# Layer 1's modulation weights in a staging ring of their own, taken in pairs of column chunks

## The chip, the cores and the metric

The kernel runs on one core of a Trainium2 chip. The metric is device time in microseconds (us): from the first to the last instruction of one execution, as a median over several runs. Names of engines: PE is TensorE, DVE is VectorE, ACT is ScalarE, POOL is GpSimd, SP is SyncE, which here only issues DMAs.

## The reference

Two layers of a trunk work on 256 latent and 256 context tokens of width 2048, all in float32. Layer 0 mixes tokens by pooling windows, layer 1 by neighbourhood attention; each is followed by a gated feed-forward block of width 5504. Before each sub-layer the tokens are normalised and modulated, and the modulation is what the change is about:

```python
silu_c, silu_cc = jax.nn.silu(c), jax.nn.silu(c_ctx)
for i in range(DEPTH):                                     # DEPTH = 2
    ml = (silu_c  @ w_mod[i] + b_mod[i]).reshape(B, 6, 1, D)   # for the latent tokens
    mc = (silu_cc @ w_mod[i] + b_mod[i]).reshape(6, 1, 1, D)   # for the context tokens
    a_lat = modulate(rms_norm(h, norm1_g[i]), ml[:, 0], ml[:, 1])
    a_ctx = modulate(rms_norm(hc, norm1_g[i]), mc[0], mc[1])
    ...                                                    # mixer i
    h = h + ml[:, 2] * y_lat
    h = h + ml[:, 5] * conv_ffn(modulate(rms_norm(h, norm2_g[i]), ml[:, 3], ml[:, 4]), ...)
    if not last:
        ...                                                # the same for the context tokens hc
```

`w_mod[i]` is 2048 by 12288 and is read once per layer: 24 chunks of 512 columns, 4 MB each. Of layer 1 the first 8 chunks (shift and scale of the first norm) are needed for both streams, and the other 16 for the latent tokens alone.

## The kernel before, in words

The program is written in order, and a scheduler that simulates its time line sets the order of the instructions on each engine; every engine then runs its own list strictly in that order. So does SP: a DMA that waits for a free buffer holds up all DMAs behind it.

Float32 products are made on PE as three passes. A weight tile of 128x1024 float32 (512 KB) is loaded into a staging buffer; ACT copies it, rounded, to a tile `h` (line 142), DVE subtracts that to get the remainder, tile `l` (line 144), and PE multiplies `h` and `l` with the two halves of the activations. I call the copy and subtraction of one tile its split. Split tiles lie in a ring of three pairs plus one (`whp`, `whx`), so the tile that is split for PE lies at most three tiles ahead of the one that PE reads.

Staging buffers come from one pool of six (`wst`), which `load` and `stage` hand out in turn to whatever asks next. While a buffer is in use, the load that is to come into it waits on SP.

The feed-forward block of layer 0 fills the span from about 450 to 1760 us. It runs over 43 slices `f` of 128 columns; the products of the first eight are made during the mixer. From the ninth on, `gu0(f)` makes the gate and up products (lines 651 to 653), with two tiles `wg` and two tiles `wu`, and `gate0` turns them into an activation `act` (lines 337 to 352). After four slices, `down0` multiplies the four slices before those with the down weights (lines 675 to 677), in four groups `mg` of two tiles `wd`; ACT scales the result into `dy` (line 687) and POOL adds it to the residual `hl`, `hc` (line 688). A period of four slices and one down step is 24 weight tiles.

Beside that block, DVE computes the modulation of layer 1. `mod_pieces` is a generator of 96 pieces, and `gu0` and `down0` draw one at each pair of weight tiles (`next(pump)`). A piece loads two tiles `wm` through the same staging pool and does on DVE, for each of four rows of 128 inputs, `macc = wm * c + macc` (lines 219 and 221), 128x512, for one stream or for both. After four pieces a chunk is summed: DVE transposes blocks of 32 and reduces them (lines 228 and 229, tile `modr`), PE sums the four quarters with one matmul with a constant tile `quad` (line 165, `modt`), and DVE adds the bias (line 181). That matmul is issued with high priority in the midst of the block's matmuls.

In layer 0 the same weights go through PE (`mod_pe`), also out of the staging pool.

Of the kernel before, what the change touches and what calls it, by code (L numbers as in the profile page):

```python
# [34 lines left out]
RATE = 20  # L35
PMAX = 30

NRH = 3
# [19 lines left out]
def kernel(ctx: ExitStack, tc: tile.TileContext, xT, cxT, wmod, wg, wu, wd, wp,  # L58
                         wq, wv, wo, vec, cc, rope, inv, strips, out):
    nc = tc.nc  # L60
    main = ctx.enter_context(tc.tile_pool(name="main", bufs=1))
    wst = ctx.enter_context(tc.tile_pool(name="wst", bufs=6))
    whp = ctx.enter_context(tc.tile_pool(name="whp", bufs=3))
# [41 lines left out]

    rooms = [None] * 6

    def lend(ks):

        rooms[:] = [r for r in rooms if r is None or r in ks] + [k for k in ks if k not in rooms]  # L110

    def stage(name):

        r = rooms.pop(0)
        rooms.append(r)
        if r is not None:
            return ap0.tile([P, 1024], F32, tag=f"A{r}", name=name)
        return wst.tile([P, 1024], F32, tag="wst", name=name)

# [39 lines left out]

    def quarter_sum(x, n, name):  # L160


        with tc.high_priority():
            ps = bank("d", f"{name}s")
            nc.tensor.matmul(ps[:, : 16 * n].rearrange("p (k s) -> p k s", s=n), quad, x, start=True, stop=True)
        v = ps[:, : 16 * n].rearrange("p (i b s) -> p i b s", b=4, s=n)
        return [v[32 * b : 32 * b + 32, :, b, :] for b in range(4)]

    def finish_mod(l, ch, streams, src):

        mt = src[0] if len(src) == 1 else main.tile([P, 4, 2], F32, name=f"modT{l}_{ch}")
        n = len(streams)
        which, q = divmod(ch, 4)

        def dup(name, a):
            return V(name)[:, a : a + 8].rearrange("p (i s) -> p i s", s=2)[:, :, 0:n]

        bias = dup(f"bm_{l}", 8 * ch)
        for b, v in enumerate(src):
            own = slice(32 * b, 32 * b + 32) if len(src) > 1 else slice(0, P)  # L180
            nc.vector.tensor_tensor(mt[own, :, 0:n], v, bias[own], op=ALU.add)
        if which in (1, 4):
            nc.vector.scalar_tensor_tensor(mt[:, :, 0:n], mt[:, :, 0:n], 1.0, dup(f"g{1 if which == 1 else 2}_{l}", 8 * q),
                                           op0=ALU.add, op1=ALU.mult)
        modT[l, ch] = mt

    def mod_pe(l, ch, sc, pool):

        ps = bank("m", f"mod{l}_{ch}")
        for g in range(4):  # L190
            ts = load(lambda a, b: wmod[l, ch, g, :, a:b], 2048, f"wm{l}_{ch}_{g}")
            for j in range(4):
                nc.tensor.matmul(ps[32 * j : 32 * j + 32, :], sc[:, 4 * g + j, :],  # L193
                                 ts[j // 2][0][:, 512 * (j % 2) : 512 * (j % 2) + 512],
                                 start=(g == 0), stop=(g == 3), tile_position=(0, 32 * j))
            if g == 3:
# [9 lines left out]
        finish_mod(l, ch, both, [r])  # L206

    def mod_pieces(todo, pool):

        for l, ch, streams in todo:  # L210
            acc = {s: pool.tile([P, 512], F32, tag=f"macc{s}", bufs=1, name=f"macc{s}_{l}_{ch}") for s in streams}
            for g in range(4):
                ts = load(lambda a, b: wmod[l, ch, g, :, a:b], 2048, f"wm{l}_{ch}_{g}")
                for j in range(4):
                    k = 4 * g + j
                    w = ts[j // 2][0][:, 512 * (j % 2) : 512 * (j % 2) + 512]
                    for s in streams:
                        if k == 0:
                            nc.vector.tensor_scalar(acc[s], w, sc2[:, k, s : s + 1], None, op0=ALU.mult)
                        else:  # L220
                            nc.vector.scalar_tensor_tensor(acc[s], w, sc2[:, k, s : s + 1], acc[s],  # L221
                                                           op0=ALU.mult, op1=ALU.add)
                if g == 3:
                    n = len(streams)
                    r = pool.tile([P, 16, 2], F32, tag="modr", bufs=2, name=f"modr_{l}_{ch}")[:, :, 0:n]
                    for s in streams:
                        t = f0.tile([P, 512], F32, tag="t2", name=f"modu{s}_{l}_{ch}")
                        nc.vector.transpose(t, acc[s])
                        nc.vector.tensor_reduce(out=r[:, :, s], in_=t.rearrange("p (k r) -> p k r", r=32), axis=AX.X,
                                                op=ALU.add)  # L230
                yield
            finish_mod(l, ch, streams, quarter_sum(r, n, f"modt_{l}_{ch}"))

# [62 lines left out]
    with ExitStack() as ph0:  # L296
# [16 lines left out]
        PART = {}  # L313
        sc = p0.tile([P, KT, 32], F32, name="sc")
        nc.gpsimd.memset(sc, 0.0)
        nc.vector.tensor_copy(sc[:, :, 0:2], sc2)
        wsh = p0.tile([P, 2, NS, 2], F32, name="wsh")
# [17 lines left out]
        def gate0(f, pg, pu):  # L335
# [10 lines left out]
            if f == NS - 1:  # L346
                a = [mp.tile([P, 512], F32R, tag=f"macc{j}", bufs=1, name=f"act_{f}_{j}") for j in range(2)]
            else:
                a = act_tile(f"act_{f}", F32R)
                a = [a[:, 0], a[:, 1]]  # L350
# [8 lines left out]
        with ExitStack() as phs:  # L359
            st = phs.enter_context(tc.tile_pool(name="st", bufs=2, reuse_waits="tile"))  # L360
            for g in range(4):
                nc.sync.dma_start(hl[:, 4 * g : 4 * g + 4, :], xT[:, 4 * g : 4 * g + 4, :])
# [272 lines left out]
        extra.append(whx)  # L635
        two = [(1, q, both) for q in range(8)]
        one = [(1, q, (0,)) for q in range(8, 24)]
        pump = mod_pieces([x for t in zip(two, one[::2], one[1::2]) for x in t], mp)
# [20 lines left out]
        def down0(c, fs, acts, after=None):  # L659
            n = len(fs)  # L660
            last = c == len(chunks) - 1
            for mg in range(4):
                parts = split(load(lambda a, b: wd[0, mg, :, fs[0] + a // 512 : fs[0] + b // 512, :], 512 * n, f"wd0_{c}_{mg}"),
                              f"wd0_{c}_{mg}")
                if c > 1:
                    next(pump, None)
                    if mg % 2 and c < 3:
                        next(pump, None)
                for m in range(4):
# [48 lines left out]
        down0(*prev)  # L718
        for _ in pump:
            pass  # L720
        extra.clear()

# [506 lines left out]
```

## Time and profile before

| | |
|---|---|
| three runs | 3149.84, 3158.88, 3161.52 us; median 3158.88 |
| span of the profiled execution | 3167.2 us, 8.3 us above that median (no other time of that execution is given) |
| PE busy | 3058.2 us (97%), 15082 matmuls |
| DVE busy | 2031.6 us (64%) |
| ACT, POOL busy | 1364.5 us (43%), 940.3 us (30%) |
| bytes moved | 559.72 MB, 177 GB/s over the span |

The shares are those of the whole span, in which stages with other limits lie. PE's busy time counts matmuls that overlap, so what counts of PE is the time in which it has none: some 109 us in all. The windows that follow are in us from the span's start.

### The profile page before, as it was taken

How to read it: one execution, taken by the hardware profiler on the slowest of the kernel's cores; microseconds unless marked ns; L12 is line 12 of the kernel's file. 1: busy time of each engine (PE TensorE's matmuls, PEld its weight loads, DVE VectorE, ACT ScalarE, POOL GpSimd, SP SyncE). 2: the span in 40 equal slices, each digit the busy share in tenths (PEclk: the TensorE clock that was granted, in tenths of full speed). 3: DMA queues.
4: the chain of work that ended last, by engine and by line, in shares of the span. 5: the costliest groups of instructions: out<-in, count | busy, mean ns of one | idle time of the engine just before them, and what ended most of it. 6: DMA issues, size and time to landing. Idle time of an engine off the chain costs nothing.

```text
span 3167.2 us, 40924 instructions
## 1 busy us (share of the span) xinstructions
PE 3058.2 (97%) x15082; PEld 2419.7 (76%) x15082; DVE 2031.6 (64%) x2865; ACT 1364.5 (43%) x2219; POOL 940.3 (30%) x846
## 2 busy tenths in 40 slices
PE   5999999999999999999999999999999999999998
PEld 2565558887877777777778788778778888888887
DVE  4444774287685876758585674564777666666666
ACT  3333454323233332323234453343545655556665
POOL 2011213204042240404133000000002477667776
PEclk9999999999999999999999999999999999999999
DMA  9877663265564656555464233333345555555553
GB/s 360 322 283 278 214 225 102 90 226 181 178 195 159 204 160 204 163 185 189 159 205 132 95 119 103 104 108 101 108 140 180 178 193 180 199 184 183 180 185 115
DMA packets 161545, 559.72 MB, mean 177 GB/s; under 512 B 17600, under 2 KB 22208, under 8 KB 161344
## 3 DMA queue, kind: packets, MB, share of 16 engines
q1 hardware_dynamic: 161344, 557.10, 53.2%
q8 instruction: 119, 1.95, 0.2%
q14 instruction: 82, 0.67, 0.1%
HBM read 554.93 MB, written 2.10 MB: 176 GB/s over the span
## 4 chain that ended last, share of the span: by engine, by line
PE 69%; DMA 13%; DVE 11%; issue 3%; POOL 3%; ACT 1%; SPq 0%; DVEq 0%; POOLq 0%; ACTq 0%
DMA wm<-wmod 12%; DVE macc L221 5%; PE g L781 5%; PE u L781 4%; PE d L826 4%; PE d L677 3%; PE mod L193 3%; PE d L675 3%; PE d L676 3%; PE g L782 2%; PE u L782 2%; PE d L827 2%; PE k L951 2%; PE q L969 2%; PE k L953 2%
## 5 line engine op out<-in xcount | busy, mean ns | idle before, releaser
L221 DVE SCALAR_TENSOR_TENSOR macc<-wm,sc,macc 128x512 f32<-128x512 f32 x480 | 410.0, 878 | 231.8 <-DMA wm<-wmod 227.3
L688 POOL TENSOR_TENSOR hl<-hl,dy 128x256 f32<-128x256 f32 x160 | 163.7, 1023 | 941.9 <-ACT dy L687 941.0
L838 POOL TENSOR_TENSOR hl<-hl,dy 128x256 f32<-128x256 f32 x320 | 321.3, 1037 | 45.4 <-ACT dy L836 43.8
L687 ACT ACTIVATE dy<-d,modT 128x256 f32<-128x256 f32 x320 | 133.2, 470 | 172.2 <-PE d L677 157.0
L688 POOL TENSOR_TENSOR hc<-hc,dy 128x256 f32<-128x256 f32 x160 | 179.8, 1124 | 0.0
L344 ACT ACTIVATE sg<-g 128x512 f32<-128x512 f32 x43 | 27.2, 632 | 309.3 <-DVE g L341 309.3
L193 PE MATMUL mod<-wm,sc 128*32 128x512 f32 x768 | 137.3, 632 | 22.4 <-DVE n1q L255 19.3
L925 POOL TENSOR_TENSOR rk<-rk,rp 128x256 f32<-128x256 f32 x16 | 13.8, 861 | 366.0 <-DVE rk L924 302.4
L836 ACT ACTIVATE dy<-d,modT 128x512 f32<-128x512 f32 x160 | 103.6, 686 | 29.9 <-PE d L827 27.5
L428 POOL TENSOR_TENSOR pf<-ws,inv 128x256 f32<-128x256 f32 x32 | 26.4, 847 | 208.7 <-DVE ws L420 187.7
L144 DVE TENSOR_TENSOR wd_2l<-wd,wd_2h 128x1024 fp32r<-128x1024 f32 (+1 forms) x44 | 57.5, 1312 | 47.0 <-ACT wd_2h L142 46.1
L677 PE MATMUL d<-act,wd_0l 128*128 128x512 f32 x172 | 71.0, 413 | 16.4 <-DVE wd_0l L144 16.4
L805 DVE TENSOR_TENSOR actb<-sgb,actb 128x256 fp32r<-128x256 f32 x43 | 70.0, 1628 | 21.1 <-ACT actb L804 20.3
L193 PEld LDWEIGHTS mod<-wm,sc 128*32 128x32 f32 x768 | 23.5, 111 | 76.9 <-issue 63.0
L144 DVE TENSOR_TENSOR wd_0l<-wd,wd_0h 128x1024 fp32r<-128x1024 f32 (+1 forms) x44 | 54.3, 1235 | 34.0 <-ACT wd_0h L142 33.3
L1011 ACT ACTIVATE sb<-sb,nm 128x512 f32<-128x512 f32 x64 | 46.2, 722 | 63.1 <-DVE nm L1007 61.4
L142 ACT CAST wd_0h<-wd 128x1024 fp32r<-128x1024 f32 (+1 forms) x44 | 45.3, 1031 | 63.4 <-PE g L652 32.2
L676 PE MATMUL d<-act,wd_0h 128*128 128x512 f32 x172 | 70.0, 407 | 0.0
L675 PE MATMUL d<-act,wd_0h 128*128 128x512 f32 x172 | 69.7, 406 | 0.0
L677 PE MATMUL d<-act,wd_1l 128*128 128x512 f32 x172 | 68.1, 396 | 0.5 <-DVE wd_1l L144 0.5
L676 PE MATMUL d<-act,wd_2h 128*128 128x512 f32 x172 | 68.0, 395 | 0.0
L675 PE MATMUL d<-act,wd_3h 128*128 128x512 f32 x172 | 68.0, 395 | 0.0
(1762 smaller groups left out, 10063.2 us busy)
## 6 DMA issues: line engine op xcount, KB each, us to landing
wm<-wmod SPq DMA_DIRECT2D x384, 512.0 KB, 5.4
wd<-wd SPq DMA_DIRECT2D x168, 512.0 KB, 4.6
wg<-wg SPq DMA_DIRECT2D x156, 512.0 KB, 4.2
wu<-wu SPq DMA_DIRECT2D x156, 512.0 KB, 4.8
wv<-wv SPq DMA_DIRECT2D x32, 512.0 KB, 3.7
wk<-wq SPq DMA_DIRECT2D x32, 512.0 KB, 3.9
wq<-wq SPq DMA_DIRECT2D x32, 512.0 KB, 3.8
wo<-wo SPq DMA_DIRECT2D x32, 512.0 KB, 3.8
```

Source lines behind the costliest of these rows:

```text
L144: eng.tensor_tensor(lo[:, :n], t[:, :n], hi[:, :n].bitcast(F32), op=ALU.subtract)
L193: nc.tensor.matmul(ps[32 * j : 32 * j + 32, :], sc[:, 4 * g + j, :], ts[j // 2][0][:, 512 * (j % 2) : 512 * (j % 2) + 512], start=(g == 0) ...
L221: nc.vector.scalar_tensor_tensor(acc[s], w, sc2[:, k, s : s + 1], acc[s], op0=ALU.mult, op1=ALU.add)
L675: nc.tensor.matmul(ps, hi[:, o : o + P], xh, start=(i == 0), stop=False)
L676: nc.tensor.matmul(ps, hi[:, o : o + P], xl, start=False, stop=False)
L677: nc.tensor.matmul(ps, lo[:, o : o + P], xh, start=False, stop=(i == n - 1))
L687: nc.scalar.activation(y[:, s], ps[:, T * s : T * s + T], AF.Copy, scale=M(0, 5, k, s))
L688: nc.gpsimd.tensor_tensor(h_of(s)[:, k, :], h_of(s)[:, k, :], y[:, s], op=ALU.add)
L781: nc.tensor.matmul(ps, hi[:, c : c + P], flat(B[k]), start=(k == 0), stop=False)
L782: nc.tensor.matmul(ps[:, T:], lo[:, c : c + P], B[k][:, 0], start=False, stop=(k == KT - 1))
L826: nc.tensor.matmul(ps, hi[:, o : o + P], flat(acts[i]), start=(i == 0), stop=False)
L838: nc.gpsimd.tensor_tensor(hl[:, k, :], hl[:, k, :], y[:, q], op=ALU.add)
```

## The change

The six staging tiles become two rings of three in the same pool: tag `wst` for block weights, tag `wm` for layer 1's modulation weights. In layer 0's mixer and from the attention on, `stage` still walks through all six; from the first `pump()` until the modulation is done, block weights have the three of `wst` alone.

Of the 24 chunks, the first 8 (both streams) still go one at a time (`single`): eight tiles of 128x1024, four DVE instructions of 128x512 per tile. The other 16 go two at a time (`pair`): a tile now holds 512 columns of two chunks for one row of inputs, and one DVE instruction of 128x1024 takes it. The DVE instructions for the products go from 512 to 384, the loads stay 192 of 512 KB. One single and one pair alternate.

Each draw from the generator no longer yields one piece of two tiles: `pump()` adds 2.9 to an account, and draws tiles that cost 1.0 (pair) or 2.3 (single) until it is used up.

The transposed sums of all chunks are kept in one tile `sums`, and the matmul with `quad` is done twice at the end (`spread`, 128x256 each), not 24 times. The bias is then added by 12 DVE instructions in place of 96. The results lie in one tile `m1`.

The padded input `sc` for layer 0's modulation moves to a pool that is closed earlier, and the two accumulators `macc0`, `macc1` become one tile of twice the width.

```diff
-    wst = ctx.enter_context(tc.tile_pool(name="wst", bufs=6))
+    wst = ctx.enter_context(tc.tile_pool(name="wst", bufs=3))
...
-    rooms = [None] * 6
+    rooms = ["wst"] * 3 + ["wm"] * 3
...
-    def mod_pieces(todo, pool):
-
-        for l, ch, streams in todo:
-            acc = {s: pool.tile([P, 512], F32, tag=f"macc{s}", bufs=1, name=f"macc{s}_{l}_{ch}") for s in streams}
...
-            finish_mod(l, ch, streams, quarter_sum(r, n, f"modt_{l}_{ch}"))
+    def mod_pieces(pool):
+
+        sums = pool.tile([P, 32, 16], F32, name="modr")
...
+        def pair(a):
+
+            acc = pool.tile([P, 2, 512], F32, tag="macc", bufs=1, name=f"macc_{a}")
+            for k in range(KT):
+                t = wst.tile([P, 1024], F32, tag="wm", name=f"wm1_{a}_{k}")
+                w = t.rearrange("p (c n) -> p c n", c=2)
+                g, kk = divmod(k, 4)
+                nc.sync.dma_start(w, wmod[1, a : a + 2, g, :, 512 * kk : 512 * kk + 512].rearrange("c p n -> p c n"))
...
+                    nc.vector.scalar_tensor_tensor(acc, w, sc2[:, k, 0:1], acc, op0=ALU.mult, op1=ALU.add)
+                yield 1.0
+            for c in range(2):
+                fold(acc[:, c], a + c + 8, f"{a + c}")
...
+        def single(ch):
...
+                    yield 2.3
...
+        for n in range(8):
+            yield from single(n)
+            yield from pair(8 + 2 * n)
+        yield 0.5
+        spread(0, 16, 0, "modt_a")
+        spread(16, 16, 8, "modt_b")
+        yield 0.5
...
+        def pump():
+
+            rooms[:] = ["wst"] * 3
+            owed[0] += PACE
+            while owed[0] > 0.0:
+                owed[0] -= next(pieces, 1e9)
...
                 if c > 1:
-                    next(pump, None)
-                    if mg % 2 and c < 3:
-                        next(pump, None)
+                    pump()
```

On SP, the loads at the end of slice 23 and the start of the down step that follows (`wd_4` is its weight tile, `wm_13` and `wm_3` are modulation chunks) stood like this before:

```order
L126 DMA wu_23_0_7466<-wu 128x1024
L126 DMA wu_23_1024_7468<-wu 128x1024
L126 DMA wm_13_1_0_7478<-wmod 128x1024
L126 DMA wm_13_1_1024_7480<-wmod 128x1024
L126 DMA wd_4_0_0_7545<-wd 128x1024
L126 DMA wd_4_0_1024_7547<-wd 128x1024
L126 DMA wm_13_2_0_7557<-wmod 128x1024
L126 DMA wm_13_2_1024_7559<-wmod 128x1024
L126 DMA wd_4_1_0_7637<-wd 128x1024
L126 DMA wd_4_1_1024_7639<-wd 128x1024
```

Two and two alternate there. In the changed kernel the same place reads as follows (`wm_12_3` is the fourth of the sixteen tiles of the pair of chunks 12 and 13):

```order
L127 DMA wd_4_0_0_7411<-wd 128x1024
L215 DMA wm_12_3_7343<-wmod 128x2x512
L127 DMA wd_4_0_1024_7413<-wd 128x1024
L215 DMA wm_12_4_7346<-wmod 128x2x512
L215 DMA wm_12_5_7349<-wmod 128x2x512
L215 DMA wm_12_6_7423<-wmod 128x2x512
L127 DMA wd_4_1_0_7504<-wd 128x1024
L215 DMA wm_12_7_7426<-wmod 128x2x512
L215 DMA wm_12_8_7429<-wmod 128x2x512
L127 DMA wd_4_1_1024_7506<-wd 128x1024
L215 DMA wm_12_9_7516<-wmod 128x2x512
L215 DMA wm_12_10_7519<-wmod 128x2x512
```

Here two or three modulation tiles stand between one weight tile and the next, and the tiles of a pair stand close together: seven weight tiles ahead of `wm_12_3` have none between them.

On DVE, around the splits of the first two `wd_4` tiles, before:

```order
L144 TENSOR_TENSOR wu_23l_7475<-wu_23_1024_7468,wu_23h_7474 128x1024
L221 SCALAR_TENSOR_TENSOR macc_1_13_7408<-wm_13_3_0_7649,sc_81,macc_1_13_7408 128x512
L352 TENSOR_TENSOR act_7386<-sg_7383,act_7386 128x512
L221 SCALAR_TENSOR_TENSOR macc_1_13_7408<-wm_13_3_1024_7651,sc_81,macc_1_13_7408 128x512 x2
L144 TENSOR_TENSOR wd_4_0l_7550<-wd_4_0_0_7545,wd_4_0h_7549 128x1024
L219 TENSOR_SCALAR macc_1_3_7753<-wm_3_0_0_7754,sc_81 128x512
L144 TENSOR_TENSOR wd_4_0l_7554<-wd_4_0_1024_7547,wd_4_0h_7553 128x1024
L221 SCALAR_TENSOR_TENSOR macc_1_3_7753<-wm_3_0_0_7754,sc_81,macc_1_3_7753 128x512
L339 SCALAR_TENSOR_TENSOR g_23_7535<-g_23_7417,vt,g_23_7535 128x2x255
```

And in the changed kernel:

```order
L145 TENSOR_TENSOR wu_23l_7340<-wu_23_1024_7333,wu_23h_7339 128x1024
L384 TENSOR_TENSOR act_7251<-sg_7248,act_7251 128x512
L219 SCALAR_TENSOR_TENSOR macc_7272<-wm_12_4_7346,sc_81,macc_7272 128x1024
L219 SCALAR_TENSOR_TENSOR macc_7272<-wm_12_5_7349,sc_81,macc_7272 128x1024
L145 TENSOR_TENSOR wd_4_0l_7416<-wd_4_0_0_7411,wd_4_0h_7415 128x1024
L219 SCALAR_TENSOR_TENSOR macc_7272<-wm_12_6_7423,sc_81,macc_7272 128x1024
L219 SCALAR_TENSOR_TENSOR macc_7272<-wm_12_7_7426,sc_81,macc_7272 128x1024
L219 SCALAR_TENSOR_TENSOR macc_7272<-wm_12_8_7429,sc_81,macc_7272 128x1024
L145 TENSOR_TENSOR wd_4_0l_7420<-wd_4_0_1024_7413,wd_4_0h_7419 128x1024
L370 SCALAR_TENSOR_TENSOR g_23_7401<-g_23_7282,vt,g_23_7401 128x2x255
```

One or two 128x512 instructions between two splits have become two or three of 128x1024; the row stands so from the splits of `wu_23` to those of `wd_4_2`, and behind them come five splits in a row.

On PE, at the end of the block, the last of the 24 small matmuls stood within a down step:

```order
L677 MATMUL d_9_3_2_12821<-act_11457,wd_9_3l_12770 128x512
L675 MATMUL d_9_3_2_12821<-act_11613,wd_9_3h_12769 128x512
L676 MATMUL d_9_3_2_12821<-act_11613,wd_9_3h_12769 128x512
L165 MATMUL modt_23s<-modr_23_12781,quad 128x16
L677 MATMUL d_9_3_2_12821<-act_11613,wd_9_3l_12770 128x512
```

The two that remain stand one group into the last down step:

```order
L715 MATMUL d_10_0_3_12580<-act_12134,wd_10_0h_12517 128x512
L716 MATMUL d_10_0_3_12580<-act_12134,wd_10_0l_12518 128x512
L248 MATMUL modt_a<-modr,quad 128x256
L248 MATMUL modt_b<-modr,quad 128x256
L714 MATMUL d_10_1_0_12626<-act_11833,wd_10_1h_12600 128x512
```

Elsewhere in the block PE's order is unchanged. In layer 0's mixer, some of the modulation matmuls stand a few rows later or earlier, and in the attention many of the score matmuls and transposes do; which instructions there are does not change.

More of the change, by code (lines that the diff above doesn't have):

```diff
@@ L36 @@
 PMAX = 30
+PACE = 2.9
 NRH = 3
@@ L104 @@
     hold = []
-    rooms = [None] * 6
+    rooms = ["wst"] * 3 + ["wm"] * 3
     def lend(ks):
-        rooms[:] = [r for r in rooms if r is None or r in ks] + [k for k in ks if k not in rooms]
+        rooms[:] = [r for r in rooms if r in ("wst", "wm") or r in ks] + [k for k in ks if k not in rooms]
     def stage(name):
@@ L115, in stage @@
         rooms.append(r)
-        if r is not None:
-            return ap0.tile([P, 1024], F32, tag=f"A{r}", name=name)
-        return wst.tile([P, 1024], F32, tag="wst", name=name)
+        if r in ("wst", "wm"):
+            return wst.tile([P, 1024], F32, tag=r, name=name)
+        return ap0.tile([P, 1024], F32, tag=f"A{r}", name=name)
     def load(src, cols, name):
@@ L158, in by_row, with finish_mod @@
         return ps.rearrange("p (i j c) -> p i c j", i=4, j=4)[:, :, 0:2, :]
[L160 to L172, printed above, removed]
-        which, q = divmod(ch, 4)
[L175 to L181, printed above, removed]
+    def finish_mod(l, ch, mt):
+        which, q = divmod(ch, 4)
+        mt2 = flat(mt)
+        nc.vector.tensor_tensor(mt2, mt2, V(f"bm_{l}")[:, 8 * ch : 8 * ch + 8], op=ALU.add)
         if which in (1, 4):
-            nc.vector.scalar_tensor_tensor(mt[:, :, 0:n], mt[:, :, 0:n], 1.0, dup(f"g{1 if which == 1 else 2}_{l}", 8 * q),
+            nc.vector.scalar_tensor_tensor(mt2, mt2, 1.0, V(f"g{1 if which == 1 else 2}_{l}")[:, 8 * q : 8 * q + 8],
                                            op0=ALU.add, op1=ALU.mult)
@@ L346, in gate0 @@
             if f == NS - 1:
-                a = [mp.tile([P, 512], F32R, tag=f"macc{j}", bufs=1, name=f"act_{f}_{j}") for j in range(2)]
+                a = mp.tile([P, 2, 512], F32R, tag="macc", bufs=1, name=f"act_{f}")
+                a = [a[:, 0], a[:, 1]]
             else:
@@ L360 @@
             st = phs.enter_context(tc.tile_pool(name="st", bufs=2, reuse_waits="tile"))
+            sc = st.tile([P, KT, 32], F32, bufs=1, name="sc")
+            nc.gpsimd.memset(sc, 0.0)
+            nc.vector.tensor_copy(sc[:, :, 0:2], sc2)
             for g in range(4):
@@ L635 @@
         extra.append(whx)
-        two = [(1, q, both) for q in range(8)]
-        one = [(1, q, (0,)) for q in range(8, 24)]
-        pump = mod_pieces([x for t in zip(two, one[::2], one[1::2]) for x in t], mp)
+        pieces = mod_pieces(mp)
+        owed = [0.0]
+        def pump():
[3 more added lines that the diff above has]
+                owed[0] -= next(pieces, 1e9)
         def gu0(f):
@@ L665, in down0 @@
                 if c > 1:
[L666 to L668 removed]
+                    pump()
                 for m in range(4):
@@ L718 @@
         down0(*prev)
-        for _ in pump:
+        for _ in pieces:
             pass
+        rooms.extend(["wm"] * 3)
         extra.clear()
```

65 lines of the change are left out of this document (42 added, 23 removed).

## The prediction

> **What bounds the kernel now.** I read the page first, then the block's stretch by windows, then PE's waits in it, then the chain of waits there, and the loads last. Of the page the engines' rows and the costliest group count:
>
> ```profile
> PE 3058.2 (97%) x15082; PEld 2419.7 (76%) x15082; DVE 2031.6 (64%) x2865; ACT 1364.5 (43%) x2219; POOL 940.3 (30%) x846
> L221 DVE SCALAR_TENSOR_TENSOR macc<-wm,sc,macc 128x512 f32<-128x512 f32 x480 | 410.0, 878 | 231.8 <-DMA wm<-wmod 227.3
> ```
>
> PE is the bound, so only time in which PE has nothing, or runs slowly, can be won. DVE's largest group is the modulation, and before it DVE stood idle for 227.3 us for modulation tiles. The windows of the block and of the attention (columns as for the page's engines, then granted clock, share of the DMA engines, GB/s):
>
> ```profile
> 600.00:1700.00 1100.00, 1065.03 (x4597) 866.02 (x4596) 778.82 (x987) 354.96 (x546) 283.51 (x262) 0.99 0.56 181
> 1800.00:2300.00 500.00, 500.00 (x2490) 401.56 (x2490) 296.05 (x592) 215.22 (x376) 26.80 (x31) 1.00 0.35 108
> ```
>
> In the attention PE lacks nothing; in the block it lacks 35.0 of 1100 us, and its clock is 1% short. What PE waited for from 560 to 1700 us (us in total, times, longest):
>
> ```profile
> PE d L677 <- DVE wd_0l L144: 16.4, 6, 3.7
> PE modt_1s L165 <- DVE modr L229: 4.5, 1, 4.5
> PE g L653 <- DVE wg_36l L144: 1.8, 1, 1.8
> PE g L653 <- DVE wg_24l L144: 1.7, 1, 1.7
> PE modt_5s L165 <- DVE modr L229: 1.7, 1, 1.7
> PE modt_7s L165 <- DVE modr L229: 1.6, 1, 1.6
> PE g L653 <- DVE wg_20l L144: 1.4, 1, 1.4
> PE g L653 <- DVE wg_28l L144: 1.3, 1, 1.3
> PE modt_2s L165 <- DVE modr L229: 1.1, 1, 1.1
> PE modt_4s L165 <- DVE modr L229: 1.1, 1, 1.1
> PE modt_3s L165 <- DVE modr L229: 1.1, 1, 1.1
> PE modt_20s L165 <- DVE modr L229: 0.7, 1, 0.7
> PE d L677 <- DVE wd_1l L144: 0.5, 1, 0.5
> ```
>
> That is 34.9 us, all of it for DVE: 16.9 for splits of down weights, 6.2 for splits of gate weights just after a down step, 11.8 for the reduced sums that the small `quad` matmul takes. Why are splits late on an engine that is idle a quarter of the time? The chain of waits ahead of the down step at 864 us says it (start, length, what):
>
> ```profile
> 829.53 1.23 DVE wg_19l L144
> 830.78 4.89 DMA wm<-wmod
> 836.44 1.23 DVE wg_19l L144
> ...
> 856.89 1.23 DVE wd_0l L144
> 858.13 4.51 DMA wm<-wmod
> 863.07 1.23 DVE wd_0l L144
> 864.34 0.50 PE d L677
> ```
>
> Split, load of a modulation tile, split, load: the split frees a buffer of the common ring, a modulation tile comes into it, and since its products stand ahead of the next split on DVE, the split waits for that load. From 829.53 to 863.07 are five rounds of 6.7 us. PE's timeline gives what PE needs per tile:
>
> ```profile
> 859.63 0.39 PE L651 MATMUL u<-A,wu_19h 128*128 128x512 f32 x1
> 863.06 0.40 PE L675 MATMUL d<-act,wd_0h 128*128 128x512 f32 x1
> ```
>
> These two starts are 15 matmuls apart, 0.229 us each, so the 24 of a tile take 5.5 us. Each round loses 1.2 us against PE, until the lead is spent and PE waits.
>
> **The change part by part.** The sum is made against the profiled execution's span, 3167.2 us; that lies 8.3 us over the median of 3158.9, and I take the difference over to the median.
>
> *The rings.* A load `wm` now waits only for products on DVE, not for a split, and a weight load only for a split three tiles back. What could make splits late now is the burst: up to three products between two splits, for five tiles. Its prices:
>
> ```profile
> wm<-wmod SPq DMA_DIRECT2D x192, 512.0 KB, 4.7
> L221 DVE SCALAR_TENSOR_TENSOR macc<-wm,sc,macc x480: 734/752/1337, 636.0 to 1697.9; 128x512 f32<-128x512 f32 x160
> L352 DVE TENSOR_TENSOR act<-sg,act 128x512 fp32r<-128x512 f32 x31 | 21.7, 701 | 0.0
> L144 DVE TENSOR_TENSOR wd_0l<-wd,wd_0h 128x1024 fp32r<-128x1024 f32 x16 | 19.5, 1219 | 0.0
> L142 ACT CAST wd_0h<-wd 128x1024 fp32r<-128x1024 f32 (+1 forms) x44 | 45.3, 1031 | 63.4 <-PE g L652 32.2
> ```
>
> The first row is the median landing in the block. A product of 128x1024 isn't in the trace: doubling the width took a subtraction from 0.70 to 1.22 us, so 0.75 becomes about 1.27 us (estimate; at least the 1.22 of a split, at most twice the longest product, 2.7, beside POOL, and the burst stands mostly ahead of the down step, where POOL adds). A ring of three gives three tiles per landing and product, 4.7 + 1.27 = 6.0 us, against 5.5 us of PE: 0.5 lost per tile, 2.5 over five tiles. The lead is three tiles, 16.5 us, less the copy of 1.03 and the split of 1.22: 14.2 us. So the burst uses a sixth of it, and five splits in a row behind it give it back. In the single stage three tiles wait loaded, and between two splits stand at most six products of 128x512, 6 x 0.75 = 4.5, plus 1.22: about PE's 5.5. The exception is the first tile of `wu` after a down step, behind two reductions and eleven products at up to 1.34: some 15 us once, 10 more than a tile of PE, inside the lead again. Both `wg` splits there now stand ahead of all these, which is where the four waits of 6.2 us came from. I take 23.1 us of waits down to 2: **21 us won**. Ends: all 23.1, or a loss as in the rivals.
>
> *The small matmuls.* Twenty-two go. What the 24 cost, and the nearest row for a width of 256:
>
> ```profile
> 600.00:1700.00 1100.00, 7.51 (x46) 8.29 (x46) 0.99 0.56 181
> L551 PE MATMUL pwg<-wcg,sh x128: 376/379/403, 98.0 to 413.6; 128*32 128x256 f32 x128
> ```
>
> The first row is line 165 alone: 46 records, two per matmul, 7.5 us. The two new ones make four records, at 0.38 some 1.5 us: **6.0 us won** (5 to 7.5). Their waits, 11.8 us in seven, become one wait for the last reduction; at the mean of the seven, 1.7: **10.1 us won** (11.8 at best; 7.3 with the longest, 4.5). The 12 additions, and two banks held until they are done, stand in the last down step behind a split; they replace what stood there, and I cost them at nothing. If they were late, PE would miss a bank there once, for the time of one split.
>
> *The clock.* The granted clock falls to half after PE has waited:
>
> ```profile
> 1003.60:1007.00 3.40, 3.02 (x7) 2.44 (x8) 2.40 (x4) 0.87 (x2) 0.00 (x0) 0.50 0.44 153
> 1471.30:1474.70 3.40, 3.40 (x9) 2.64 (x8) 3.40 (x5) 0.00 (x0) 0.42 (x1) 0.50 0.66 229
> ```
>
> Such a stretch holds 7 to 9 matmuls in place of 15. The block's 0.99 is 11 us of 1100. If the waits go, most of these go; I take **6 us won** (0 to 11), as some waits remain. The Trainium skill (TensorE: Matmul & The Clock Gate, Part 1) says that the clock is halved after an idle window of about 3.4 us and released after a busy one as long. By that rule waits of the size I leave would not trip it, all 11 us would come back, and the sum would be 5 us better. The trace agrees on the length, 3.4 us at 0.50, but the second row follows a wait of 1.8 us (`wg_36l`), shorter than that window.
>
> *What moves elsewhere.* The attention and layer 0's mixer get another order with the same instructions. PE has no idle time from 1800 to 2300 us, so a new order can only lose: **2 us lost** (0 to 10; 10 us would be 2% of those 500). DVE's shorter list itself (128 fewer product instructions, 84 fewer additions) lies beside PE and wins nothing. The bytes and the number of loads stay.
>
> Sum: 21 + 6.0 + 10.1 + 6 - 2 = 41 us. 3167.2 - 41 = 3126 for such an execution; 3158.9 - 41 = **3118 us** for the median.
>
> **The rivals.**
>
> *The burst runs into the loads.* Four tiles per 5.5 us are 381 GB/s. The stage from 60 to 420 us, where traffic is dense, shows what loads take then:
>
> ```profile
> GB/s 392 209 386 297 275 401 111 366 411 322 302 54 124 344 394 392 300 326 350 240 197 354 329 109 269 396 226 332 396 273 104 238 0 155 201 252 332 173 317 274
> wm<-wmod SPq DMA_DIRECT2D x147, 512.0 KB, 6.5
> wcg<-wg SPq DMA_DIRECT2D x16, 512.0 KB, 7.7
> wp<-wp SPq DMA_DIRECT2D x6, 512.0 KB, 8.0
> ```
>
> The rate has been reached in single slices. At a landing of 6.5 us the round is 7.8, 2.3 lost per tile, 11.5 in five: still within 14.2. The lead is spent at 14.2 / 5 = 2.8 lost per tile, a landing of 7.1 us. `wcg`, which like a pair comes in runs of 512 columns, took 7.7: 3.5 lost per tile, 17.4 in five, 3.2 us of PE per burst, 25 us in eight bursts: the 23.1 us are lost again, with the clock. Then only 10.1 + 6 - 2 + 23.1 - 25 = 12 us are won: 3147 us. For it speaks the shape, against it that it was measured amid slices near 400 GB/s, while the block moves 181 and the bursts fill a fifth of it.
>
> *SP becomes the bound (slower).* SP issues in order: in the burst, `wd_4_1_0` stands behind `wm_12_6`, which waits for products on DVE, so a late modulation tile also delays the weights, of which only three tiles are staged, not up to six. With landings beyond those 8.0, say 9.3 us (5.1 lost per tile, 25.4 in five), each burst costs PE 11 us, eight 89: 3158.9 - 14 + 89 - 23 = 3211 us. It decides against the change, by over 16 us, from about 6.7 us per burst, a landing of 8.4. The 4.7 us of the block is far from that, and so are the 8.0 of the dense stage.
>
> *The new order elsewhere eats it.* If the moved scores and transposes make PE wait in the attention, as much as 28 us in some 500, the time is 3145 us. Against it: PE's 500.00 of 500, with DVE at 296 and the loads at 0.35 there.
>
> **How the numbers follow.** Forecast 0.75, landings 0.12, SP 0.06, the other order 0.07. The low end is all 23.1 + 11.8 + 7.5 + 11 = 53 us won, 3106; the high end 3148 takes in the first and the third rival, and leaves out the second and little below. A difference under 0.5% (16 us: 3143 to 3175) could not be told from none. The forecast counts as faster but for 0.02; the cases at 3145 and 3147 lie just above the bound of 3143, so about half of their 0.19 falls on either side: faster 0.82, same 0.12, slower 0.06.
>
> **What would show it.** Right: in the block PE's waits for `wd` and `wg` splits under 5 us, one wait at most for the two `modt` matmuls, the clock at 1.00, the block some 40 us shorter (each period of 24 tiles by about 5), no chain through `wm` loads, and the attention as long as before.
>
> Wrong: waits for `wd` splits in the middle of the down step, `wm` landings over 7 us in the bursts, SP waiting long for `macc` with weight loads behind it, or PE idle from 1800 to 2300 us.

## The result, and the profile after

The changed kernel took 3114.92 us (median of 4 runs, 3110.03 to 3116.34) against 3160.2 us for the kernel before: a ratio of 0.9866, 95% interval 0.985 to 0.9883, 45 us less. The forecast was 3118 us. The profiled execution of after has a span of 3112.2 us, 55.0 less than that of before. The two are not alike among their runs. A listed time is 1.8 us longer than the span of the same execution (3114.03 and 3112.2 for after), so the profiled execution of before took some 3169.0 us: 8.8 above the 3160.2, the median of four runs, and 10.1, not 8.3, above the 3158.88 of the first three. That of after lies 0.9 below its median.

First the engines' row and the two groups of products from DVE's list by shape, 600 to 1700 us:

```profile
PE 3037.3 (98%) x15038; PEld 2406.4 (77%) x15038; DVE 1946.2 (63%) x2647; ACT 1370.8 (44%) x2219; POOL 896.1 (29%) x846
```

```profile
L238 DVE SCALAR_TENSOR_TENSOR macc<-wm,sc,macc 128x512 f32<-128x512 f32 x240 | 186.2, 828 | 0.0
L219 DVE SCALAR_TENSOR_TENSOR macc<-wm,sc,macc 128x1024 f32<-128x1024 f32 x120 | 158.5, 1321 | 63.8 <-DMA wm<-wmod 62.6
```

DVE now waits 62.6 us for modulation tiles of pairs, and 0.0 ahead of the single ones; before it was 227.3 us at line 221, and 50.2 more ahead of the first product of a chunk (line 219). The wide product takes 1.32 us on average. The windows that were read before:

```profile
600.00:1700.00 1100.00, 1100.00 (x4788) 899.87 (x4787) 729.53 (x827) 388.36 (x602) 253.95 (x282) 1.00 0.60 187
1800.00:2300.00 500.00, 494.87 (x2505) 395.43 (x2504) 305.35 (x614) 212.91 (x376) 24.82 (x28) 1.00 0.35 108
```

In the block PE has work in 1100.00 of 1100 us, where it lacked 35, and the clock is 1.00. The second window is not like for like: the attention moved 55 us ahead, and its end now lies in the window. In the same stretch of before, 1855 to 2355 us, PE has work in 495.35 of 500, so the attention is as it was. The longest of PE's waits in the whole span, and the shares of the chain by engine, of after:

```profile
PE mod L177 <- DVE n1q L289: 19.9, 1, 19.9
PE modt L187 <- ACT modev L182: 12.0, 5, 5.1
PE n3b L306 <- DVE n3d L304: 2.6, 1, 2.6
```

```profile
PE 94%; POOL 2%; DVE 2%; issue 1%; DMA 1%; ACT 1%; SPq 0%; DVEq 0%; POOLq 0%; ACTq 0%
```

No wait for a split and none for reduced sums is left in the block; the first two rows belong to layer 0, and the third lies behind the block. Loads in the block (last number: median us from issue to landing):

```profile
wm<-wmod SPq DMA_DIRECT2D x191, 512.0 KB, 5.6
wd<-wd SPq DMA_DIRECT2D x68, 512.0 KB, 5.6
```

Modulation tiles land 0.9 us later than before (4.7). Apart, the single tiles (line 230) have a median of 4.8 and those of pairs (line 215) one of 5.9. From the start of the first to the start of the last of the block's own matmuls (those of `wg`, `wu` and `wd` from slice 8 on) the two traces give 1302.0 us before and 1247.4 after: 54.6 of the span's 55.0 us were won there. I call this the block's length below.

### The profile page after: what moved, and what is told of

Same layout as the page of the kernel before. It is cut to its first block, busy times and chain, and to the rows that moved or that the text cites. A ratio compares the mean times of both kernels' runs of the same rounds, so it can differ in the third digit from the quotient of the medians.

```text
span 3112.2 us, 40670 instructions
## 1 busy us (share of the span) xinstructions
PE 3037.3 (98%) x15038; PEld 2406.4 (77%) x15038; DVE 1946.2 (63%) x2647; ACT 1370.8 (44%) x2219; POOL 896.1 (29%) x846
## 4 chain that ended last, share of the span: by engine, by line
PE 94%; POOL 2%; DVE 2%; issue 1%; DMA 1%; ACT 1%; SPq 0%; DVEq 0%; POOLq 0%; ACTq 0%
PE g L821 5%; PE d L714 5%; PE d L716 5%; PE d L715 5%; PE u L821 5%; PE d L866 4%; PE u L692 4%; PE u L693 4%; PE u L694 4%; PE g L692 4%; PE g L694 4%; PE g L693 4%; PE mod L177 3%; PE g L822 3%; PE u L822 2%; PE d L867 2%
## 5 line engine op out<-in xcount | busy, mean ns | idle before, releaser
L727 POOL TENSOR_TENSOR hl<-hl,dy 128x256 f32<-128x256 f32 x160 | 144.7, 905 | 933.4 <-ACT dy L726 932.5
L878 POOL TENSOR_TENSOR hl<-hl,dy 128x256 f32<-128x256 f32 x320 | 322.1, 1040 | 45.3 <-ACT dy L876 43.7
L219 DVE SCALAR_TENSOR_TENSOR macc<-wm,sc,macc 128x1024 f32<-128x1024 f32 x120 | 158.5, 1321 | 63.8 <-DMA wm<-wmod 62.6
L238 DVE SCALAR_TENSOR_TENSOR macc<-wm,sc,macc 128x512 f32<-128x512 f32 x240 | 186.2, 828 | 0.0
L727 POOL TENSOR_TENSOR hc<-hc,dy 128x256 f32<-128x256 f32 x160 | 150.6, 941 | 0.0
L145 DVE TENSOR_TENSOR wd_3l<-wd,wd_3h 128x1024 fp32r<-128x1024 f32 (+1 forms) x33 | 40.5, 1230 | 69.2 <-ACT wd_3h L143 69.2
L143 ACT CAST wd_1h<-wd 128x1024 fp32r<-128x1024 f32 (+1 forms) x44 | 45.2, 1029 | 58.2 <-PE u L693 33.5
L714 PE MATMUL d<-act,wd_1h 128*128 128x512 f32 x172 | 68.1, 396 | 0.0
```

The source lines that it names most:

```text
L219: nc.vector.scalar_tensor_tensor(acc, w, sc2[:, k, 0:1], acc, op0=ALU.mult, op1=ALU.add)
L238: nc.vector.scalar_tensor_tensor(acc[:, s], w, sc2[:, k, s : s + 1], acc[:, s], op0=ALU.mult, op1=ALU.add)
L714: nc.tensor.matmul(ps, hi[:, o : o + P], xh, start=(i == 0), stop=False)
L727: nc.gpsimd.tensor_tensor(h_of(s)[:, k, :], h_of(s)[:, k, :], y[:, s], op=ALU.add)
L878: nc.gpsimd.tensor_tensor(hl[:, k, :], hl[:, k, :], y[:, q], op=ALU.add)
```

## Experiments: which part does it

Twelve kernels ran, three rounds each or more. Each ratio is to the kernel before, timed on the same chip (medians from 3153.7 to 3157.0 us). The lines of code are cut to what differs.

**The sums at the end, alone.** Old pieces, old ring of six shared tiles; `modr` of all chunks is kept and PE sums it twice at the end. (The run is made out of the changed kernel, and also has its one tile for the accumulators and its 12 additions of the bias.)

```diff
 # in the kernel before
-            finish_mod(l, ch, streams, quarter_sum(r, n, f"modt_{l}_{ch}"))   # 24 times
+        spread(0, 16, 0, "modt_a")                                            # once, at the end
+        spread(16, 16, 8, "modt_b")
```

> The kernel before with only the sums of the last step moved: pieces of two tiles from the common ring of six, 128x512 products, but the 24 small quad matmuls become two at the end. If the prediction's terms are right (ring and small matmuls are separate), it wins the 11.8 us of waits for the reduced sums, some 6 us of matmuls and a part of the clock, about 20 us: 3140 us, and PE still waits about 23 us for splits of wd and wg. Rival, that the small matmuls set off the late splits too (they take the high-priority places on DVE and PE): the waits for splits go as well and it comes to about 3120.

Measured: 3176.49 against 3155.81 us, ratio 1.0066 (1.0042 to 1.009): 21 us longer, which neither expectation had. PE's waits for the first down splits in it:

```profile
PE d L696 <- DVE wd_0l L145: 38.2, 7, 7.3
```

The waits for reduced sums are gone, but those for splits rose from 23 to 43 us. So the waits for sums seem to be no cost of their own: in a kernel whose splits come too late, PE waits for the one or for the other. This is argued and not shown, because the scheduler also turned round the two halves of thirty block weights in SP's order, so this run is not the batch and nothing else.

**The rings, alone.** The kernel before, with three tiles for block weights and three for modulation.

```diff
 # in the kernel before
+                rooms[:] = ["wm"] * 3
                 ts = load(lambda a, b: wmod[l, ch, g, :, a:b], 2048, f"wm{l}_{ch}_{g}")
+                rooms[:] = ["wst"] * 3
```

> The kernel before with nothing but the two rings of three: pieces of two tiles, one per draw, 128x512 products and 24 small matmuls stay. New theory, after the shared ring with another pace was as fast as the changed kernel: what made splits late is that two weight tiles and two modulation tiles alternate, four tiles walking through six buffers, so that every modulation load follows a split and every weight load a product. Rings of their own end that at the old pace too: waits for wd and wg splits from 23 us to under 5, while the waits for the reduced sums and the 24 matmuls stay: about 3130 us. Rival, that pace and place of the products do it and the rings nothing: 3155 to 3160 us, waits for splits near 23 us.

Measured: 3122.84 against 3153.71 us, 0.9898 (0.9878 to 0.9917). Its block's window, and the only wait for DVE's work left in the block:

```profile
600.00:1700.00 1100.00, 1098.67 (x4805) 899.01 (x4804) 802.78 (x1032) 384.96 (x595) 281.49 (x282) 1.00 0.57 186
```

```profile
PE modt_1s L165 <- DVE modr L231: 1.3, 1, 1.3
```

The rings take away the late splits, the half clock, and also 10.5 of the 11.8 us of waits for reduced sums, though all 24 small matmuls are still there.

What this run does not separate is the buffers from the order that comes with them. The scheduler knows the rings and places the products otherwise: in most periods DVE's list has one and three products between the first three splits of a down step in the kernel before, and none among the first six with the rings. With the new pace below, products do stand there (up to nine between two splits in the runs without pairs) and no split is late, so such an order is not enough to make them late.

**Rings and sums at the end**, with the old pieces and products of 128x512:

> The kernel before with the rings of three and the sums in two batches, old pace and 128x512 products. By the new theory the late splits go by the rings, the other waits by the batches: 3115 us, as the changed kernel. Rival, that pace is needed as well: waits for splits of 15 us or more and 3135 us or more.

Measured: 3111.53 us, 0.9868 (0.9852 to 0.9883): as fast as the changed kernel, with neither pairs nor the new pace. Against the rings alone the block is 6.5 us shorter (1253.9 to 1247.4), 1.3 of it the wait above; the other 5.2 I put down to the work of the small matmuls. The medians differ by more, 11.3 us; in the profiled pair 4.6 us lie ahead of the block.

**The changed kernel without its rings.** All loads of the block take turns in six shared tiles; pairs, pace and sums at the end stay.

```diff
 # in the changed kernel
-                t = wst.tile([P, 1024], F32, tag="wm", name=f"wm1_{a}_{k}")
+                t = stage(f"wm1_{a}_{k}")
...
-            rooms[:] = ["wst"] * 3
```

> The changed kernel, but its modulation tiles come out of the common ring of six like the weights; pairs, pace and the two batches stay. If the ring of its own is what took the late splits away, the waits for wd and wg splits come back with about 15 to 25 us and half-clock stretches with them: 3135 to 3145 us, and the chain shows split, load, split again. Rival, that pairs and pace did it (fewer, denser products in another place): waits under 5 us, 3115 us.

Measured: 3113.28 against 3155.81 us, 0.9869 (0.9855 to 0.9884). I had expected it to lose what the rings win, and it lost nothing. All that PE waited for splits in it:

```profile
PE d L715 <- DVE wd_2l L145: 1.0, 1, 1.0
```

DVE, however, waits for modulation tiles three times as long as in the changed kernel, 186 us where that had 62.6:

```profile
DVE macc L219 <- DMA wm<-wmod: 166.8, 58, 6.5
DVE macc L238 <- DMA wm<-wmod: 19.4, 12, 2.8
```

**The same with single chunks only** (pace by tile, sums at the end, six shared tiles, no pair):

> Only draws by tile with the pace of 2.9 and the two batches; the ring of six is shared, all chunks single. In a single stage about five modulation tiles go with four pairs of weights, so four in six does not recur. By the new theory it is as fast as the changed kernel, 3115 us, with waits for splits under 5 us. Rival, that in the shared-ring run the pairs were what helped: 3130 us or more, split and load in turn in the chain.

Measured: 3115.71 against 3153.71 us, 0.9876 (0.9858 to 0.9895). So the pace with the sums at the end removes the late splits as well as the rings do. In the run with the sums alone, the pieces came two tiles at a time and the splits were later than ever; by that comparison it is the pace. The reservation on that run weighs less here: in the two runs with the pace and six shared tiles the scheduler also turned round the halves of 13 and 15 block weights, and their splits are in time.

**The changed kernel without pairs**, all chunks single, DVE with 512 products of 128x512 again:

> The changed kernel with all 24 chunks taken singly (one-stream chunks with two 128x512 products per tile, cost 1.0), own rings and batches kept. The prediction gave the pairs nothing, since DVE lies beside PE: 3115 us, no waits for splits. Rival, that the saved DVE time is what lets splits be early: some 10 us of waits and 3125 us or more.

Measured: 3113.88 against 3155.81 us, 0.9868 (0.9852 to 0.9883), no split wait in the block. Its modulation loads:

```profile
wm<-wmod SPq DMA_DIRECT2D x192, 512.0 KB, 4.8
wd<-wd SPq DMA_DIRECT2D x68, 512.0 KB, 4.2
```

Pairs win nothing. That `wm` and `wd` of the changed kernel land later, at 5.6, goes with the pairs: without them they take 4.8 and 4.2.

**A small matmul after each chunk**, in the changed kernel:

```diff
 # in the changed kernel, at the end of pair (and of single)
+            for c in range(2):
+                finish(a + c)          # bank, matmul with quad, bias, for this chunk
```

> The changed kernel, but each chunk's small quad matmul and bias as soon as the chunk is summed, 24 matmuls as before; rings, pairs and pace stay. By the prediction's terms it gives back 6 us of matmuls and waits for the reduced sums, 10 us if they are as long as before: 3120 to 3132 us. Rival, that these waits too came from loads that held up DVE through the common ring: only the 6 us, 3121 us, with waits near nothing.

Measured: 3161.82 us, 1.0022 (1.0012 to 1.0031): all was lost, and both expectations were missed, by some 30 us at the least. The chain ahead of a wait says why (start, length, what):

```profile
1034.73 1.14 DVE wu_24l L145
1035.87 1.33 DVE macc L254 x2
1038.53 2.03 DVE macc L254 x3
...
1053.07 1.22 DVE wu_24l L145
1054.33 0.50 PE u L691
```

The scheduler had put the split of the second half of `wu_24` ahead of that of the first, which PE needs first, with 17 products between the two, and so in seven periods. The same edit with the matmul issued some tiles into the next chunk keeps the halves in order:

> The changed kernel with one small matmul per chunk again, but issued two (pairs) or two tiles (singles) into the next chunk; in the earlier run of this kind the scheduler had put the second half of seven wu splits ahead of the first, with up to 17 products between, and this one has all halves in order. If that swap was the cost, this gives back only the 6 us of matmuls and some of the waits for reduced sums: 3121 to 3127 us, no waits for splits. Rival, that small matmuls in the midst of the block cost as such what that run showed: 3150 us or more.

Measured: 3125.87 against 3153.71 us, 0.9912 (0.9894 to 0.993), one wait of PE for sums:

```profile
PE modt_22s L213 <- DVE modr L206: 3.6, 1, 3.6
```

So most of what the first version lost is the cost of an order that the scheduler happened to choose, not of the matmuls: its block is 34 us longer than this one's, 20 of them PE's waits for gate and up splits and 12 half clock. With a small matmul per chunk in this order the block takes 1259.0 us in place of 1247.4. Of the 11.6 us, 3.6 are the wait above, 3.4 are lost in the 6.8 us of half clock behind it, and 4.6 are left for the matmuls.

## Experiments: why either the rings or the pace is enough

With six tiles every cure looks complete, so the next ones take tiles away.

**Four shared tiles**, old pieces, old sums. I had a finer theory by then: two weight tiles and two modulation tiles by turns in a ring of six always pass a buffer to the other kind, in a ring of four always to their own.

```diff
 # in the kernel before, for the block alone
-    rooms = [None] * 6
+    rooms = ["wst"] * 4 + ["wm"] * 2
...
+                rooms[:] = ["wst"] * 4           # from the first modulation tile on
```

> The kernel before, but from the first modulation tile on all loads of the block draw from one common ring of four staging tiles (two tiles lie idle there; elsewhere all six as before). Theory by place in the ring: two weight tiles and two modulation tiles are drawn by turns, so a ring of six gives each buffer to the other kind each time and ties split to load to split, while a ring of four gives each buffer back to its own kind: with fewer buffers the waits for down and gate splits fall under 5 us and the time to 3115 to 3135 us. Rival by room: sharing as such, or too few tiles ahead, makes the loop, and four are worse than six: split waits above 40 us, block clock at or under 0.99, 3165 to 3250 us. About even before the run.

Measured: 3317.08 against 3154.74 us, 1.0511 (1.0495 to 1.0526). The theory by place in the ring fell; room counts, and more than the rival had said (3165 to 3250). The window, DVE's longest wait (up to 1760 us; to the block's end, at 1902, it is 371.5), and two of PE's:

```profile
600.00:1700.00 1100.00, 993.30 (x4123) 798.46 (x4122) 672.33 (x869) 316.92 (x486) 224.58 (x231) 0.95 0.49 161
```

```profile
DVE macc L222 <- DMA wm<-wmod: 335.4, 110, 5.9
...
PE d L678 <- DVE wd_1l L144: 15.2, 6, 3.0
PE modt_12s L165 <- DVE modr L230: 8.3, 1, 8.3
```

Only some 30 us of PE's waits are for splits (the rival had said more than 40); the sums of twenty chunks take 89. Half clock fills 130 us of this block, against 23.9 before.

**Two and two**: the same four tiles, two for each kind.

```diff
 # in the run with the rings alone
-    rooms = ["wst"] * 3 + ["wm"] * 3
+    rooms = ["wst"] * 2 + ["wm"] * 2 + ["wx"] * 2     # wx lies idle in the block
...
```

> The kernel before with two rings of two staging tiles in the block (one for the block's weights, one for modulation), two more tiles idle there; all else as before. Theory by sharing (a modulation load that takes the buffer which a split has freed ties the split to that load; in a ring of their own the modulation loads wait for products only): two and two do nearly as well as three and three, 3120 to 3145 us, split waits under 10 us, although the room is that of the four shared tiles that took 3317. Rival by room (the number of tiles loaded ahead is all that counts): as with four shared tiles, above 3250 us. I hold the first at three in four.

Measured: 3161.38 against 3157.02 us, 1.0014 (1.0001 to 1.0027). Sharing, with as many tiles, costs 156 us, 143 of them in the block. The number I gave, 3120 to 3145, was missed. PE's longest waits and DVE's:

```profile
PE modt_6s L165 <- DVE modr L231: 3.9, 1, 3.9
PE modt_7s L165 <- DVE modr L231: 3.5, 1, 3.5
PE modt_3s L165 <- DVE modr L231: 3.4, 1, 3.4
...
DVE macc L223 <- DMA wm<-wmod: 120.0, 99, 3.1
```

There is no wait for a split at all: rings of their own cut that tie with only two tiles each. Late weights alone do not explain the difference, since ACT waited as long for weight tiles to land in both blocks (140 us here, 142 with four shared). The order differs here too: no product stands among the first six down splits in most periods, two in each of the first four gaps with four shared. What is left, 24 us in eight waits, is that products wait for loads, and the sums are late for the small matmul that stands at a fixed place on PE. Behind these waits the clock is at half for 34 us, 17 lost; together 41 us, against the 39 by which this block is longer than with three and three.

**Four shared tiles with the new pace** and pairs and sums at the end:

```diff
 # in the changed kernel
-            rooms[:] = ["wst"] * 3
+            rooms[:] = ["wst"] * 4
...
-                t = wst.tile([P, 1024], F32, tag="wm", name=f"wm1_{a}_{k}")
+                t = stage(f"wm1_{a}_{k}")        # modulation tiles too come from the four
```

> The changed kernel (pairs, pace by tile, sums at the end), with one common ring of four staging tiles in the block, in place of three and three. Theory that the new pace alone cures a shared ring: near 3113 to 3130 us, as with six shared tiles. Rival (the pace only needs less room, since modulation tiles no longer come two at a time; four shared tiles tie splits to loads again): 3160 to 3300 us, with modulation loads waited for by DVE for over 200 us in the block and split waits over 30 us. I hold the rival at two in three.

Measured: 3162.87 against 3157.02 us, 1.0021 (1.0005 to 1.0038), as the rival had it. DVE's waits and the three longest of PE's:

```profile
DVE macc L219 <- DMA wm<-wmod: 239.4, 81, 6.5
DVE macc L238 <- DMA wm<-wmod: 80.9, 31, 5.5
...
PE d L716 <- DVE wd_1l L145: 8.9, 4, 4.1
PE d L716 <- DVE wd_2l L145: 7.3, 4, 2.9
PE d L716 <- DVE wd_0l L145: 7.3, 3, 2.9
```

So the pace does not untie loads from splits: DVE waits for loads in both runs with a shared ring and this pace, 186 us with six tiles and 320 with four. It needs less room (four tiles at the old pace took 3317 us), and six are enough. With four the late splits are back, 29 us of waits, where the rival had said more than 30.

**Slow loads**: the changed kernel, every modulation tile loaded twice, the second load behind the first.

```diff
 # in the changed kernel
+                for _ in range(2):
                     nc.sync.dma_start(w, wmod[1, a : a + 2, g, :, ...])
```

> The changed kernel, each modulation tile loaded twice into the same buffer, the second load after the first has landed, so that a tile takes some 10 to 11 us in place of 5.6, with the same data. By the prediction's lead arithmetic (three tiles per landing and product, 11.5 us or so, against 5.5 us of PE per tile: 6 lost per tile, 30 in five, 14.2 of lead) each of eight bursts costs PE some 16 us: 3115 + 125 = 3240 us, waits for wd splits over 80 us. Rival: the products behind a late tile are few enough (192 tiles in 1250 us, one per 6.5 us, while a ring of three at 11.5 gives one per 3.8), so the late tiles are taken up elsewhere and the loss is small: 3115 to 3140 us, split waits under 20 us. The rate over the block rises from 187 to some 270 GB/s in both.

Measured: 3193.02 against 3154.74 us, 1.0123 (1.0107 to 1.014). The longest of PE's waits, and the loads of two kinds:

```profile
PE d L718 <- DVE wd_0l L145: 19.9, 10, 3.7
PE d L716 <- ACT dy L728: 10.2, 4, 3.5
PE d L718 <- DVE wd_2l L145: 8.8, 6, 3.1
...
wm<-wmod SPq DMA_DIRECT2D x367, 512.0 KB, 6.2
wd<-wd SPq DMA_DIRECT2D x61, 512.0 KB, 7.2
```

At 2 x 6.2 us per tile PE does lose time: by the two ratios, 1.0123 and 0.9866, some 80 us against single loads. In the block, 40 of them are PE's waits for splits, 10 its waits for `dy`, and 29 are lost in 58 us of half clock. Neither expectation held: the arithmetic of the lead had 125 us, and with the measured 12.4 us per tile it would give some 215; the rival had 25 at most.

Nor is it the burst alone that costs. SP waited 509 us for the first of two loads to land, and the weights stand behind these on SP. They came late as well: `wd` landed in 7.2 us in place of 5.6, and ACT waited 211 us for weight tiles, 2 in the changed kernel. So slow modulation tiles can cost PE time, but this run does not tell the rival of the burst from that of SP.

Medians in us, by tiles in the block:

| | old pieces, sums per chunk | old pieces, sums at the end | pace by tile, sums at the end |
|---|---|---|---|
| six shared | before: 3154 to 3160 | 3176 | 3113 (no pairs: 3116) |
| three and three | 3123 | 3112 | after: 3115 (no pairs: 3114) |
| four shared | 3317 | not run | 3163 |
| two and two | 3161 | not run | not run |

The five with sums at the end and six tiles, the run with the sums alone aside, lie between 3111.5 and 3115.7 us, within their intervals. None is clearly better than the changed kernel: PE waits for at most 2 us in the block in any of them.

## Why the prediction came out right, and where it did not

- *The bound.* PE, held up by late splits, over a loop of split, modulation load, split: right as far as the runs go. The late splits go when the modulation has its own tiles, even with two and two, although the order on DVE changes with the rings.
- *The rings, 21 us.* All 23.1 went. But that the rings win them is half of the story: in the changed kernel either the rings or the pace alone would have done. I had read the new rhythm of draws only as a danger (the burst).
- *The small matmuls, 6.0 us.* Rings alone against rings with sums at the end: 6.5 us of block less 1.3 of wait, so 5.2. Right, at the low end of the 5 to 7.5.
- *Their waits, 10.1 us.* 11.8 went, so the size was nearly right, but the step that gave them to the batch failed: the rings alone took 10.5 of them, and with the batch alone they went, but the waits for splits rose by 20. The two terms were not independent. That they are two places where one lateness shows fits both runs; the reservation on the second stands.
- *The clock, 6 us.* This term was mis-sized, since no wait over 1 us was left in the block. Matmuls at half speed fill 23.9 us of the block before and none after: 12 us came back. The Trainium skill (TensorE: Matmul & The Clock Gate, Part 1) ties the halving to an idle window of the clock gate; by that rule all 11 us were to come back, and they did. What that rule doesn't cover is that before, half clock followed a wait of only 1.8 us.
- *Order elsewhere, 2 us lost.* The span outside the block changed by 0.4 us. Nothing.
- *DVE's shorter list wins nothing.* Right: without pairs, with 512 products in place of 384, the time is the same.
- *The burst.* Right that it costs nothing, but its price was too low. A tile of a pair landed in 5.9 us (median; 9.1 at the longest) where the sum had 4.7; the wide product took 1.28 us (median) for the estimated 1.27. By the same arithmetic a tile loses 1.7 us, not 0.5, and five some 8, still inside the lead of 14.2. The median stayed below the 7.1 us at which the lead is spent, and PE waited for no split. SP did not become the bound.
- *The sum.* With the waits (23.1 and 11.8), the clock (12) and the matmuls (5 to 7) the profiled pair should differ by 52 to 54 us, and differs by 55. I took 41 by holding back on waits and clock. The medians differ by 45, because the profiled execution of before lay 8.8 us above its median and that of after 0.9 below. So that 3118 came within 3.1 us is partly luck: the sum was 14 us short for the pair that it was made for, and the long execution hid 10 of them.

Still open: what in the pace makes it need less room, the drawing tile by tile or its account of costs. The runs with six shared tiles show that it does, and those with four that it has a limit, but the two parts of the pace were not tried apart. Open too is how much of what the rings do is the buffers, and how much the order of products that the scheduler chooses with them.

## What to carry to other kernels

When an engine with a quarter of its time idle is late, follow the chain back to the buffer: a transfer that takes the buffer of the work it then delays is a loop, and with separate rings the late work went away here even with fewer tiles. Waits of the bottleneck engine at several places may be one lateness, so take one cause away at a time before giving each wait a price. And compare the order of instructions before you believe an ablation, since an edit to the buffers moves instructions as well: two versions of the same edit here differ by 1.1%, 35 us, because in one of them the halves of a weight had changed places.

## What was not expected of the hardware

With tiles loaded as 512 columns of two chunks, loads land later at the same 187 GB/s: `wm` at 5.6 us in place of 4.8, `wd` at 5.6 in place of 4.2, each time against the run without pairs. Within the changed kernel the tiles of pairs take 5.9 and the single ones 4.8. Whether the shorter rows do it, or that the tiles of a pair follow each other more closely, was not tried. The 128x1024 product took 1.32 us, against 0.83 for a 128x512 one in the same trace, so a doubled width cost 1.6 times, not twice; by the medians, 1.28 and 0.74, it is 1.7 times.
